# One hybrid decoder step: moving the recurrence stage's elementwise work between GpSimd, VectorE and ScalarE

## The chip, the cores and the metric

The kernel runs on one core of a Trainium2 chip. The metric is the device time in microseconds (us) of one execution, so smaller is better. Five engines work side by side and each takes its own instructions strictly in order: TensorE (PE in the rows, with its weight loads as PEld), VectorE (DVE), ScalarE (ACT), GpSimd (POOL) and SyncE (SP), which issues most of the transfers. An instruction that waits for a semaphore holds back everything behind it on its engine.

## The reference

One prompt of 512 tokens and 8 single-token samples (520 columns in all) pass a recurrent layer (HGRN2) with an MLP, then a sliding-window attention layer with an MLP. Only the recurrent layer is touched:

```python
q, f, i, g = jnp.split(h @ w_in, 4, axis=-1)
q = jax.nn.silu(q)
fg = lb + (1.0 - lb) * jax.nn.sigmoid(f)
o, S = _hgrn2_scan(heads(q), heads(1.0 - fg), heads(i), heads(jnp.log(fg)), s0)
o = _rms_norm(o, gn_g) * jax.nn.silu(heads(g))
return o.reshape(b, L, D_MODEL) @ w_out, S
# one step of the scan, for each of 8 heads of 128:
# S_new = exp(last) * S + k^T v;  o = causal part within the block + q S
```

For a sample one step of the same recurrence is taken: its stored state is scaled by the forget value, the outer product of key and value is added, the result is stored (output `hg_s`) and read by the query.

## The kernel before, in words

All matrices are fp32 and every product is made in three matmuls: weights and activations are split into an upper and a lower half, and upper x upper, upper x lower, lower x upper are added up in PSUM (`mm_half`, L229; 8 rows of 128 inputs, so 24 matmuls for each half of the columns; the two halves are 256 and 264 columns wide, in banks `ps_a` and `ps_b`). `split_w` makes the halves of a weight tile: ScalarE copies it into the rounded upper half (L179), and VectorE or GpSimd subtracts that from the raw tile to get the lower half (L180, `wsp<-wraw,wsp`, 128 x 1024 elements).

In order of time the program has a set-up (up to some 50 us), the loop over the 8 heads of the recurrence (up to some 316 us), the output gates and the output projection, a norm, the first MLP (from 404 us), attention, and the second MLP. In the loop, each head has

- `proj_head`: three weight tiles (`proj`): forget gate, query, value. The forget gate goes through a sigmoid (L422), then E = sigmoid x scale + bias (L423) and KQ = 1 - E (L424); the query through L427 and L428; the value is copied by L430. Small pieces for the samples are copied by GpSimd (L436 to L440).
- `scan_head`: the block-wise scan. VectorE doubles the block size seven times (QK in L467, E in L469); TensorE makes the small products (L449), masked into `diag` (L461, L472); ScalarE copies the pieces into `att` (L484 to L489); L491, L494, L496 turn the keys, L499 makes the states, L504 chains them, L515 and L517 make the output, and L519 to L527 normalize it: square, sum, power -0.5 on GpSimd (L523), product, and a transposition on TensorE (L527).
- after every second head `sample_pair`: the stored states of two heads for 8 samples come into one buffer, `Ss`, which exists once (L534); L541 spreads the value over the samples (`vx`); L543 scales the states; L547 and L549 add the new product; the states go out (L550); L555 to L559 make the output, L562 its square sum, L564 the power, L565 the scaling of `od`, L567 a transposition.

The order of the instructions on each engine is fixed when the program is built: a scheduler of the framework simulates the engines with its own costs and takes what is ready, so TensorE's work of the next head's projections (L229) is filled in between the small products of the scan of this head. Weights come through two raw buffers (`wraw`) and three split ones (`wsp`); the next pair's states can only be loaded into `Ss` when the last pair's have been stored and read.

Of the kernel before, what the change touches and what calls it, by code (L numbers as in the profile page):

```python
# [11 lines left out]
AF = mybir.ActivationFunctionType  # L12
ALU = mybir.AluOpType
AX = mybir.AxisListType

P = 128
# [26 lines left out]
def yoco_kernel(ctx: ExitStack, tc: tile.TileContext, I, O, dbg=None):  # L43
# [52 lines left out]
    def bc(ap, axis, n):  # L96
        a = ap.unsqueeze(axis)
        s = list(a.shape)
        s[axis] = n
        return a.broadcast_to(s)  # L100
# [106 lines left out]
    def load_w(src, raw=None):  # L207

        nk, cols = src.shape[0] // P, src.shape[1]
        raw = (wp.tile([P, 2048], F32, name="wraw") if raw is None else raw)[:, 0:nk * cols].rearrange("p (k f) -> p k f", k=nk)  # L210
        sp.dma_start(out=raw, in_=src.rearrange("(k p) f -> p k f", p=P))
        return raw

    def split_w(raw, lo_eng=None, w=None):
        nk, cols = raw.shape[1], raw.shape[2]
        if w is None:
            w = wp.tile([P, 2, 1024], F32R, name="wsp", bufs=WB)[:, :, 0:nk * cols]
        w = w.rearrange("p s (k f) -> p s k f", k=nk)
        split_into(w[:, 0], w[:, 1], raw, lo_eng)
        return w  # L220
# [164 lines left out]
    with ExitStack() as st:  # L385
# [20 lines left out]

        def proj(grp, head, act_A):
            if first and grp < 2:
                w = split_w(first.pop(0), None if grp else pool)
            else:  # L410
                w = split_w(load_w(win[:, grp * D + head * P:grp * D + (head + 1) * P]), pool)
            for h in range(2):
                yield HALVES[h], mm_half(w, act_A, h)

        def proj_head(hd):
            KQ = hg2.tile([P, 2, T], F32, name="KQ")
            E = hg2.tile([P, 2, T], F32, name="E")
            V = hg2.tile([P, T], F32, name="V")
            pool.memset(E[:, 0, 0:L], 1.0)
            for (a, b), m in proj(1, hd, A):  # L420
                s = hg2.tile([P, 264], F32, name="sg")[:, 0:b - a]
                act.activation(s, m, AF.Sigmoid)  # L422
                dve.tensor_scalar(E[:, 1, a:b], s, lbt[:, 1, hd:hd + 1], lbt[:, 0, hd:hd + 1], ALU.mult, ALU.add)  # L423
                dve.tensor_scalar(KQ[:, 0, a:b], E[:, 1, a:b], -1.0, 1.0, ALU.mult, ALU.add)  # L424
            for (a, b), m in proj(0, hd, A):
                s = hg2.tile([P, 264], F32, name="sg")[:, 0:b - a]
                act.activation(s, m, AF.Sigmoid)  # L427
                dve.tensor_tensor(KQ[:, 1, a:b], m, s, ALU.mult)  # L428
            for (a, b), m in proj(2, hd, A):
                act.copy(V[:, a:b], m)  # L430
            i, (skv, sq), fs = hd % 2, smps[hd // 2 % 2], fss[hd // 2 % 2]
            sh = hg2.tile([P, 2, NS], F32R, name="sh")
            for z, src in enumerate((KQ[:, 0, L:T], V[:, L:T])):
                hi = sh[:, z].bitcast(F32)
                g = skv[:, z, i, :, 0:NS]
                pool.tensor_copy(sh[:, z], src)  # L436
                pool.tensor_copy((g[:, 0:2], g[:, 0::2])[z], bc(hi, 1, 2))
                pool.tensor_tensor((g[:, 2:4], g[:, 1::2])[z], bc(src, 1, 2), bc(hi, 1, 2), ALU.subtract)
            pool.tensor_copy(sq[:, i, 0:NS], KQ[:, 1, L:T])
            pool.tensor_copy(fs[:, i, :], E[:, 1, L:T])  # L440
            return KQ, E, V
# [10 lines left out]
        def scan_head(h, KQ, E, V):  # L452
# [63 lines left out]
                if c:  # L516
                    pe.matmul(po[:, cs], KQ[:, 1, cs], S[:, c - 1], start=False, stop=True)  # L517
            sq = hg2.tile([P, NB, P], F32, name="osq", bufs=1)
            act.activation(sq, po.rearrange("p (c v) -> p c v", c=NB), AF.Square)  # L519
            ms = hg2.tile([P, NB], F32, name="oms")  # L520
            dve.tensor_reduce(ms, sq, axis=AX.X, op=ALU.add)
            dve.tensor_scalar(ms, ms, 1.0 / P, EPS, ALU.mult, ALU.add)
            pool.tensor_tensor(ms, ms, expo[:, 0:NB], ALU.pow)  # L523
            dve.tensor_tensor(sq, po.rearrange("p (c v) -> p c v", c=NB), bc(ms, 2, P), ALU.mult)
# [5 lines left out]
        def sample_pair(p):  # L530
            (skv, sq), fs = smps[p % 2], fss[p % 2]
            S = hg.tile([P, 2, NS, P], F32, name="Ss")
            for i in range(2):
                sp.dma_start(out=S[:, i], in_=I["state_hgrn"][0, :, 2 * p + i].rearrange("b d v -> d b v"))  # L534
            tp = ps1()
            for z in range(2):
                pe.transpose(out=tp[:, z * P:(z + 1) * P], in_=skv[:, z].rearrange("p i g b -> p (i g b)"), identity=ident)
            kT = hg2.tile([P, P], F32R, name="skT", bufs=1)
            act.copy(kT, tp[:, 0:P])
            vx = hg2.tile([P, NS, P], F32R, name="vx", bufs=1)  # L540
            dve.tensor_tensor(vx, bc(tp[:, P:2 * P], 1, NS), bc(dlt[:, 0:8], 2, P), ALU.mult)  # L541
            for i in range(2):
                pool.tensor_tensor(S[:, i], S[:, i], bc(fs[:, i], 2, P), ALU.mult)  # L543
                r = slice(64 * i, 64 * i + 64)
                for b in range(2):
                    kv = ps1()
                    pe.matmul(kv, kT[r, :], vx[r, 4 * b:4 * b + 4, :], start=True, stop=True)  # L547
                    sv = S[:, i, 4 * b:4 * b + 4, :]
                    dve.tensor_tensor(sv, sv, kv.rearrange("p (b v) -> p b v", b=4), ALU.add)  # L549
                sp.dma_start(out=O["hg_s"][0, :, 2 * p + i].rearrange("b d v -> d b v"), in_=S[:, i])  # L550
            po = ps1()
            for i in range(2):
                for b in range(2):
                    r = 64 * i + 32 * b
                    pe.matmul(po[r:r + 32, :], sq[:, i, :], S[:, i, 4 * b:4 * b + 4, :], start=True, stop=True)  # L555
            oo = hg2.tile([P, 4, P], F32, name="oo", bufs=1)
            dve.tensor_tensor(oo, po.rearrange("p (b v) -> p b v", b=4), bc(dlt[:, 8:12], 2, P), ALU.mult)
            od = hg2.tile([P, P], F32, name="od", bufs=1)
            dve.tensor_reduce(od, oo.rearrange("p b v -> p v b"), axis=AX.X, op=ALU.add)  # L559
            osq = hg2.tile([P, P], F32, name="odq", bufs=1)  # L560
            ms = hg2.tile([P, 1], F32, name="odm")
            act.activation(osq, od, AF.Square, accum_out=ms)  # L562
            dve.tensor_scalar(ms, ms, 1.0 / P, EPS, ALU.mult, ALU.add)
            pool.tensor_tensor(ms, ms, expo[:, 0:1], ALU.pow)  # L564
            dve.tensor_scalar(od, od, ms, None, ALU.mult)  # L565
            pt = ps1()
            pe.transpose(out=pt[:, 0:P], in_=od, identity=ident)  # L567
            act.activation(o32[:, 2 * p:2 * p + 2, L:T].rearrange("p i (c r) -> p i c r", c=2),
                           _ap(pt, 0, [[64, 2], [36, 2], [1, 4]]), AF.Copy, scale=GN)
# [435 lines left out]
```

## Time and profile before

| | |
|---|---|
| three runs | 1404.94, 1406.4, 1407.34 us (median 1406.4) |
| the profiled execution | 1405.58 us, of which the span from first to last instruction is 1403.8 |
| TensorE busy in the span | 1354.4 us (96%), mean granted clock 0.989 |
| VectorE, ScalarE, GpSimd busy | 819.6 us (58%), 536.1 (38%), 303.4 (22%) |
| transfers | 186 MB, 133 GB/s over the span |

The busy shares are means over stages with very different limits. The granted clock is TensorE's, as a share of full speed. Times of instructions and waits come from the one profiled execution.

### The profile page before, as it was taken

How to read it: one execution, taken by the hardware profiler on the slowest of the kernel's cores; microseconds unless marked ns; L12 is line 12 of the kernel's file. 1: busy time of each engine (PE TensorE's matmuls, PEld its weight loads, DVE VectorE, ACT ScalarE, POOL GpSimd, SP SyncE). 2: the span in 40 equal slices, each digit the busy share in tenths (PEclk: the TensorE clock that was granted, in tenths of full speed). 3: DMA queues.
4: the chain of work that ended last, by engine and by line, in shares of the span. 5: the costliest groups of instructions: out<-in, count | busy, mean ns of one | idle time of the engine just before them, and what ended most of it. 6: DMA issues, size and time to landing. Idle time of an engine off the chain costs nothing.

```text
span 1403.8 us, 29513 instructions
## 1 busy us (share of the span) xinstructions
PE 1354.4 (96%) x12459; PEld 1245.3 (89%) x12459; DVE 819.6 (58%) x1667; ACT 536.1 (38%) x1160; POOL 303.4 (22%) x315
## 2 busy tenths in 40 slices
PE   6899999899999999999999999999999999999998
PEld 4688878789889999999999966888889999999998
DVE  5676876864694443444446786777664544444432
ACT  4333333334453322322314454656454413324222
POOL 1534553353150000000000475534430000000000
PEclk9999999999999999999999999999999999999999
DMA  9744465434654552643644564113311323232231
GB/s 340 203 132 131 119 181 153 122 97 161 224 158 142 171 197 67 210 150 92 212 147 141 172 227 129 54 39 96 123 31 61 120 91 91 91 91 91 91 106 47
DMA packets 185974, 186.04 MB, mean 133 GB/s; under 512 B 6945, under 2 KB 156394, under 8 KB 185842
## 3 DMA queue, kind: packets, MB, share of 16 engines
q1 hardware_dynamic: 185600, 184.07, 41.3%
q8 instruction: 98, 1.61, 0.5%
q14 instruction: 34, 0.28, 0.1%
q10 hardware_dynamic: 242, 0.08, 0.0%
HBM read 177.00 MB, written 9.21 MB: 133 GB/s over the span
## 4 chain that ended last, share of the span: by engine, by line
PE 82%; DVE 9%; DMA 3%; issue 2%; ACT 2%; POOL 1%; SPq 0%; ACTq 0%; POOLq 0%; DVEq 0%
PE ps_b L229 34%; PE ps_a L229 32%; PE ps_a L682 4%; PE ps_e L122 3%; DVE E L469 1%; PE ps_b L768 1%; DVE QK L467 1%; PE ps_d L806 1%; DMA wraw<-in_hg_w_in_dram 1%; DVE h L187 1%; DMA adaw<-in_w_ada_dram 1%; PE ps_c L449 1%; DVE acc L155 1%; PE ps_d L499 1%; DVE X L241 1%
## 5 line engine op out<-in xcount | busy, mean ns | idle before, releaser
L229 PEld LDWEIGHTS ps_a<-A,wsp 128*128 128x128 f32 x2424 | 300.2, 192 | 28.7 <-issue 11.0
L229 PE MATMUL ps_a<-A,wsp 128*128 128x256 f32 x2424 | 319.0, 287 | 6.8 <-ACT A L193 2.6
L229 PE MATMUL ps_b<-A,wsp 128*128 128x264 f32 x2424 | 317.0, 286 | 0.8 <-DVE A L180 0.8
L229 PEld LDWEIGHTS ps_b<-A,wsp 128*128 128x128 f32 x2424 | 301.8, 189 | 10.4 <-issue 7.3
L179 ACT CAST wsp<-wraw 128x1024 fp32r<-128x1024 f32 (+1 forms) x193 | 197.9, 1027 | 284.2 <-PE ps_b L229 240.1
L180 DVE TENSOR_TENSOR wsp<-wraw,wsp 128x1024 fp32r<-128x1024 f32 (+1 forms) x159 | 193.6, 1219 | 59.9 <-ACT wsp L179 59.8
L229 PE MATMUL ps_b<-u,wsp 128*128 128x264 f32 x1536 | 200.7, 285 | 0.0
L229 PEld LDWEIGHTS ps_b<-u,wsp 128*128 128x128 f32 x1536 | 192.0, 188 | 0.1
L229 PE MATMUL ps_a<-u,wsp 128*128 128x256 f32 x1536 | 191.8, 281 | 0.1
L229 PEld LDWEIGHTS ps_a<-u,wsp 128*128 128x128 f32 x1536 | 186.0, 188 | 2.9 <-ACT u L179 2.5
L272 DVE TENSOR_TENSOR rl<-rl 128x264 f32<-128x264 f32 (+1 forms) x128 | 54.7, 428 | 135.5 <-ACT rl L271 135.5
L237 DVE SCALAR_TENSOR_TENSOR X<-ps_b,MOD,X 128x256 f32<-128x256 f32 x88 | 42.3, 481 | 135.9 <-PE ps_b L229 135.7
L171 POOL TENSOR_TENSOR rs<-rs,expo 128x2 f32<-128x2 f32 (+1 forms) x8 | 6.5, 814 | 406.1 <-DVE rs L170 401.8
L180 POOL TENSOR_TENSOR wsp<-wraw,wsp 128x1024 fp32r<-128x1024 f32 x34 | 84.1, 2475 | 32.2 <-ACT wsp L179 31.8
L237 DVE SCALAR_TENSOR_TENSOR X<-ps_a,MOD,X 128x256 f32<-128x256 f32 x88 | 42.3, 481 | 54.2 <-PE ps_a L229 54.0
L180 DVE TENSOR_TENSOR u<-rl,u 128x264 fp32r<-128x264 f32 (+1 forms) x128 | 56.8, 445 | 27.6 <-ACT u L179 27.4
L682 PE MATMUL ps_a<-wsp,u 128*128 128x256 f32 (+1 forms) x480 | 66.7, 287 | 2.1 <-ACT Vt L690 1.3
L682 PEld LDWEIGHTS ps_a<-wsp,u 128*128 128x128 f32 (+1 forms) x480 | 55.7, 168 | 12.0 <-issue 3.2
L179 ACT CAST u<-rl 128x264 fp32r<-128x264 f32 (+1 forms) x128 | 52.1, 408 | 33.7 <-DVE rl L272 33.7
L469 DVE TENSOR_TENSOR E<-E 128x512 f32<-128x512 f32 x56 | 61.0, 1090 | 0.7
L271 ACT ACTIVATE rl<-ps_a 128x256 f32<-128x256 f32 x64 | 24.5, 384 | 94.3 <-PE ps_a L229 94.3
L271 ACT ACTIVATE rl<-ps_b 128x264 f32<-128x264 f32 x64 | 25.0, 392 | 92.3 <-PE ps_b L229 92.3
(289 smaller groups left out, 1547.3 us busy)
## 6 DMA issues: line engine op xcount, KB each, us to landing
adaw<-in_w_ada_dram SPq DMA_DIRECT2D x36, 1024.0 KB
wraw<-in_w_down_dram SPq DMA_DIRECT2D x36, 1024.0 KB
wraw<-in_w_up_dram SPq DMA_DIRECT2D x32, 1024.0 KB
wraw<-in_hg_w_in_dram SPq DMA_DIRECT2D x32, 512.0 KB
wraw<-in_w_ada_dram SPq DMA_DIRECT2D x12, 1024.0 KB
wraw<-in_hg_w_out_dram SPq DMA_DIRECT2D x8, 1024.0 KB
adaw<-in_kv_w_ada_dram SPq DMA_DIRECT2D x8, 1024.0 KB
Ss<-in_state_hgrn_dram SPq DMA_DIRECT2D x8, 512.0 KB
```

Source lines behind the costliest of these rows:

```text
L122: pe.matmul(acc_ps[32 * kk:32 * kk + 32, :], cT[:, i, 4 * r + kk, :], wt[:, kk, :], start=(i == 0 and r == 0), stop=(i == n - 1 and r == 1))
L155: dve.tensor_tensor(acc[:, a:b], acc[:, a:b], sq[:, 0:b - a], ALU.add)
L179: act.copy(dst_hi, src)
L180: (lo_eng or dve).tensor_tensor(dst_lo, src, dst_hi.bitcast(F32), ALU.subtract)
L187: dve.scalar_tensor_tensor(t, X[:, j, a:a + 256], MOD[:, va, j, 8:9], rb[:, 0:256], ALU.mult, ALU.mult)
L229: pe.matmul(m[:, 0:b - a], w[:, wi, k, :], A[:, ai, k0 + k, a:b], start=(k == 0 and wi == 0 and ai == 0), stop=(k == nk - 1 and wi == 1))
L237: dve.scalar_tensor_tensor(xv, m[:, 0:256], MOD[:, vg, j, 8:9], xv, ALU.mult, ALU.add)
L241: dve.tensor_tensor(X[:, j, L:T], X[:, j, L:T], t, ALU.add)
L271: act.activation(r, m, AF.Relu)
L272: dve.tensor_tensor(r, r, r, ALU.mult)
L469: dve.tensor_tensor(_ap(E, 0, dims), _ap(E, 0, dims), tot, ALU.mult)
L682: pe.matmul(m[0:nr, 0:256], A[:, ai, k, cs], w[k][:, wi, :], start=(k == 0 and ai == 0 and wi == 0), stop=(k == KT - 1 and ai == 1))
```

## The change

Five pieces of elementwise work in the loop over heads get another engine. Nothing else of the program is edited, but the scheduler orders the engines anew.

```diff
         def proj(grp, head, act_A):
             if first and grp < 2:
-                w = split_w(first.pop(0), None if grp else pool)
+                w = split_w(first.pop(0))
             else:
-                w = split_w(load_w(win[:, grp * D + head * P:grp * D + (head + 1) * P]), pool)
+                w = split_w(load_w(win[:, grp * D + head * P:grp * D + (head + 1) * P]))
...
-                dve.tensor_scalar(E[:, 1, a:b], s, lbt[:, 1, hd:hd + 1], lbt[:, 0, hd:hd + 1], ALU.mult, ALU.add)
-                dve.tensor_scalar(KQ[:, 0, a:b], E[:, 1, a:b], -1.0, 1.0, ALU.mult, ALU.add)
+                act.activation(E[:, 1, a:b], s, AF.Identity, scale=lbt[:, 1, hd:hd + 1], bias=lbt[:, 0, hd:hd + 1])
+                act.activation(KQ[:, 0, a:b], E[:, 1, a:b], AF.Identity, scale=-1.0, bias=ones[:, 0:1])
...
-            act.activation(sq, po.rearrange("p (c v) -> p c v", c=NB), AF.Square)
-            dve.tensor_reduce(ms, sq, axis=AX.X, op=ALU.add)
+            for c in range(NB):
+                act.activation(sq[:, c], po[:, c * P:(c + 1) * P], AF.Square, accum_out=ms[:, c:c + 1])
...
-            dve.tensor_tensor(vx, bc(tp[:, P:2 * P], 1, NS), bc(dlt[:, 0:8], 2, P), ALU.mult)
+            for b in range(NS):
+                act.activation(vx[:, b], tp[:, P:2 * P], AF.Copy, scale=dlt[:, b:b + 1])
             for i in range(2):
-                pool.tensor_tensor(S[:, i], S[:, i], bc(fs[:, i], 2, P), ALU.mult)
+                for b in range(NS):
+                    act.activation(S[:, i, b], S[:, i, b], AF.Copy, scale=fs[:, i, b:b + 1])
...
-            dve.tensor_scalar(od, od, ms, None, ALU.mult)
+            act.activation(od, od, AF.Copy, scale=ms)
```

The new program has three more lines, so L543, L547, L549, L555, L562, L564, L565 and L567 of before are L545, L549, L551, L557, L564, L566, L567 and L569 of the new one.

The first place is VectorE at the start of the first head's scan. Before:

```order
L423 TENSOR_SCALAR E<-sg,lbt 128x264
L428 TENSOR_TENSOR KQ<-ps_a,sg 128x256
L424 TENSOR_SCALAR KQ<-E 128x264
L428 TENSOR_TENSOR KQ<-ps_b,sg 128x264
L467 TENSOR_TENSOR QK<-KQ,E 128x512
L469 TENSOR_TENSOR E<-E 128x256x2
L467 TENSOR_TENSOR QK<-KQ,E 128x512
L469 TENSOR_TENSOR E<-E 128x128x2x2
L461 TENSOR_TENSOR diag<-ps_c,masks 128x128
L467 TENSOR_TENSOR QK<-KQ,E 128x512
L472 COPY_PREDICATED diag<-masks,ps_c 128x128
```

Now:

```order
L428 TENSOR_TENSOR KQ<-ps_a,sg 128x256
L180 TENSOR_TENSOR wsp<-wraw,wsp 128x1024
L428 TENSOR_TENSOR KQ<-ps_b,sg 128x264
L467 TENSOR_TENSOR QK<-KQ,E 128x512
L180 TENSOR_TENSOR wsp<-wraw,wsp 128x1024
L469 TENSOR_TENSOR E<-E 128x256x2
L461 TENSOR_TENSOR diag<-ps_c,masks 128x128
L467 TENSOR_TENSOR QK<-KQ,E 128x512
L472 COPY_PREDICATED diag<-masks,ps_c 128x128
L469 TENSOR_TENSOR E<-E 128x128x2x2
L180 TENSOR_TENSOR wsp<-wraw,wsp 128x1024
```

The products of E and KQ (L423, L424) are gone from the row, three lower halves of weights (L180) stand in it, and the first masked product (L461) has one doubling step (L467, L469) ahead of it where it had two.

The second place is ScalarE after the first pair of samples (heads 0 and 1), where the square sum of the samples' output is made. Before:

```order
L528 ACTIVATE o_406<-ps_d,GT 128x512
L459 COPY vts<-ps_d 128x512
L562 ACTIVATE odq,odm<-od 128x128
L422 ACTIVATE sg<-ps_a 128x256
L568 ACTIVATE o_406<-ps_e,GT 128x2x8
L489 COPY att_426<-diag 32x4x32 x4
L422 ACTIVATE sg<-ps_b 128x264
L179 CAST wsp<-wraw 128x1024
```

Now:

```order
L528 ACTIVATE o_406<-ps_d,GT 128x512
L564 ACTIVATE odq,odm<-od 128x128
L545 ACTIVATE Ss<-Ss,fs_424 128x128 x8
L459 COPY vts<-ps_d 128x512
L545 ACTIVATE Ss<-Ss,fs_424 128x128
L567 ACTIVATE od<-od,odm 128x128
L545 ACTIVATE Ss<-Ss,fs_424 128x128 x7
L422 ACTIVATE sg<-ps_a 128x256
L570 ACTIVATE o_406<-ps_e,GT 128x2x8
```

The scaling of the samples' output (`od`, L567 now) has come to ScalarE, and so have the scalings of the next pair's states (L545, 8 for each half of `Ss`); nine of these stand ahead of the output's scaling, seven behind it and ahead of the next head's sigmoid.

The third place is TensorE in the same stretch, from the product that reads the samples' states (L555 before, L557 now) to the transposition of their output (L567, L569). Before:

```order
L555 MATMUL ps_e<-Ss,sq_416 32x512 x4
L449 MATMUL ps_c<-QK 32x32 x2
L229 MATMUL ps_a<-A,wsp 128x256 x12
L457 MATMUL ps_d<-ident,V 128x128 x4
L449 MATMUL ps_c<-QK 32x32 x32
L229 MATMUL ps_a<-A,wsp 128x256 x12
L229 MATMUL ps_b<-A,wsp 128x264 x7
L449 MATMUL ps_c<-QK 32x32 x8
L567 MATMUL ps_e<-ident,od 128x128
```

Now:

```order
L557 MATMUL ps_e<-Ss,sq_416 32x512 x4
L449 MATMUL ps_c<-KQ 32x32 x4
L527 MATMUL ps_d<-ident,osq 128x128 x4
L449 MATMUL ps_c<-KQ 32x32 x6
L449 MATMUL ps_c<-QK 32x32 x16
L229 MATMUL ps_a<-A,wsp 128x256 x19
L457 MATMUL ps_d<-ident,V 128x128 x4
L229 MATMUL ps_a<-A,wsp 128x256 x5
L229 MATMUL ps_b<-A,wsp 128x264 x4
L449 MATMUL ps_c<-QK 32x32 x32
L229 MATMUL ps_b<-A,wsp 128x264 x17
L449 MATMUL ps_c<-QK 32x32 x4
L569 MATMUL ps_e<-ident,od 128x128
```

Between the two stand 31 matmuls of the projections (L229) before and 45 now. Of the second and third pair it is 21 and 49 before, 42 and 62 now. In ScalarE's row one scaling of the next pair's states stands ahead of the output's scaling after the second pair, and six, with four squares of the norm, after the third.

## Rows read from the trace of the kernel before

**Rows 1.** Windows by stage, in us: each engine busy, instructions, granted clock, DMA
```profile
core 0: us, PE busy (x) PEld busy (x) DVE busy (x) ACT busy (x) POOL busy (x), PEclk, DMA share, GB/s
50.00:72.00 22.00, 18.96 (x301) 17.04 (x300) 16.69 (x21) 5.50 (x10) 14.23 (x13) 0.85 0.57 179
72.00:316.00 244.00, 231.85 (x3152) 203.06 (x3139) 179.50 (x299) 82.99 (x187) 110.13 (x112) 1.00 0.46 133
404.00:1403.00 999.00, 984.51 (x8169) 924.79 (x8168) 537.70 (x1181) 381.88 (x850) 136.46 (x143) 0.99 0.37 118
```

**Rows 2.** Chain that ended last, gates stage: start us, us, what
```profile
318.20 2.91 PE ps_b L229 x24
```

**Rows 3.** Waits of PE, 49 to 316 us: total us, times, longest us
```profile
PE ps_e L567 <- DVE od L565: 4.2, 2, 3.2
PE ps_d L494 <- DVE KQ L491: 2.3, 3, 1.5
PE ps_c L449 <- DVE diag L461: 2.2, 1, 2.2
PE ps_d L527 <- DVE osq L524: 1.9, 2, 1.4
PE ps_e L547 <- DVE Ss L549: 1.9, 2, 1.5
```

**Rows 4.** Groups by form, 40 to 460 us: busy us, mean ns | idle before
```profile
L180 POOL TENSOR_TENSOR wsp<-wraw,wsp 128x1024 fp32r<-128x1024 f32 x31 | 76.7, 2475 | 13.0 <-ACT wsp L179 12.7
L180 DVE TENSOR_TENSOR wsp<-wraw,wsp 128x1024 fp32r<-128x1024 f32 x22 | 27.3, 1245 | 7.4 <-ACT wsp L179 7.4
L543 POOL TENSOR_TENSOR Ss<-Ss,fs 128x1024 f32<-128x1024 f32 x8 | 16.1, 2021 | 21.0 <-DMA Ss<-in_state_hgrn_dram 20.9
L423 DVE TENSOR_SCALAR E<-sg,lbt 128x264 f32<-128x264 f32 x8 | 3.3, 413 | 11.6 <-ACT sg L422 11.6
L521 DVE TENSOR_REDUCE oms<-osq 128x4 f32<-128x512 f32 x8 | 5.4, 674 | 5.4 <-ACT osq L519 5.4
L541 DVE TENSOR_TENSOR vx<-ps_e,dlt 128x1024 fp32r<-128x1024 f32 x4 | 4.9, 1216 | 0.5 <-ACT skT L539 0.5
```

**Rows 5.** Timelines of DVE and POOL: start us, us, engine, line, operation
```profile
25.99 2.66 DVE L194 SCALAR_TENSOR_TENSOR A<-h,MOD,A 128x256 fp32r<-128x256 f32 x2 [0.85 <-ACT A L193]
32.02 0.87 DVE L194 SCALAR_TENSOR_TENSOR A<-h,MOD,A 128x256 fp32r<-128x256 f32 x2
113.92 3.37 DVE L469 TENSOR_TENSOR E<-E 128x512 f32<-128x512 f32 x1
118.42 0.69 DVE L469 TENSOR_TENSOR E<-E 128x512 f32<-128x512 f32 x1
113.91 2.39 POOL L180 TENSOR_TENSOR wsp<-wraw,wsp 128x1024 fp32r<-128x1024 f32 x1
```

**Rows 6.** Timeline around one pair of samples (heads 4 and 5)
```profile
255.42 0.38 SPq L550 DMA_DIRECT2D out_hg_s_dram<-Ss  x1
259.87 0.99 SPq L534 DMA_DIRECT2D Ss<-in_state_hgrn_dram  x2
260.32 0.31 ACT L562 ACTIVATE odq<-od 128x128 f32<-128x128 f32 x1 [5.78 <-DVE od L559]
264.88 1.90 POOL L543 TENSOR_TENSOR Ss<-Ss,fs 128x1024 f32<-128x1024 f32 x1 [15.29 <-DMA Ss<-in_state_hgrn_dram]
269.73 0.33 PE L567 MATMUL ps_e<-ident,od 128*128 128x128 f32 x1 [3.18 <-DVE od L565]
```

**Rows 7.** Single ScalarE instructions: by form, and one from the timeline
```profile
L154 ACT ACTIVATE sq<-X 128x264 f32<-128x264 f32 x7 | 2.7, 416 | 7.6 <-DVE X L241 4.2 <-DVE acc L155 3.4
L190 ACT ACTIVATE h<-h,MOD 128x256 f32<-128x256 f32 x12 | 5.9, 505 | 2.3 <-DVE h L187 2.1
L502 ACT COPY S<-ps_d 128x128 f32<-128x128 f32 x8 | 2.1, 267 | 13.8 <-PE ps_d L499 11.8 <-issue 2.0
156.49 0.19 ACT L562 ACTIVATION_READ_ACCUMULATOR odq<-od 128x1 f32 x1
```


## The prediction

> **What bounds it now.** I read the windows by stage first. From 404 us to the end TensorE is busy 984.5 of 999 us, so nothing can be won there; in the loop over heads it is busy 18.96 of 22 us (50 to 72) and 231.85 of 244 us (72 to 316), which leaves 3.04 + 12.15 = 15.2 us idle [rows 1]. That, and a lower clock in the first of the two windows, is all that the change can win in the loop. What TensorE does there isn't touched. The gates stage behind it is matmuls without a gap, 24 of them in 2.91 us (0.12 us each) in the chain that ended last [rows 2], and the order of the engines differs little there.
>
> Next, the waits of TensorE in the loop. The largest are all for VectorE: 4.2 us for the scaling of the samples' output (L565), 2.3 for the keys (L491), 2.2 for the first masked product (L461), 1.9 for the norm's product (L524), 1.9 for the states' sum (L549) [rows 3]. So VectorE is late at a few places, though it isn't full.
>
> Why it is late stands in the timelines. The doubling step L469 takes 0.69 us at 118.42, but 3.37 us at 113.92, and in that time, from 113.91, GpSimd makes a lower half (L180) for 2.39 us [rows 5]. The same is seen in the set-up: two instructions of L194 take 2.66 us at 25.99 and 0.87 at 32.02 [rows 5]. So here VectorE instructions with two operands in SBUF stand still while GpSimd reads SBUF. The Trainium skill says the same ("SBUF — State Buffer", Who interferes with whom: VectorE's second input comes through a read port shared with GpSimd, and one of the two is fully blocked for the whole instruction). By that rule the new subtractions on VectorE, which have two SBUF inputs, can in turn hold up GpSimd's short copies and powers; rival D takes that up, with a price from rows.
>
> **Part by part.**
>
> Lower halves. GpSimd makes 31 of them at 2.475 us between 40 and 460 us, 29 of them in the loop; VectorE takes 1.245 us for the same [rows 4]. So VectorE gets 29 x 1.245 = 36 us of work, and GpSimd is rid of 29 x 2.475 = 72 us. With GpSimd's state scalings (8 x 2.02 = 16 us [rows 4]) gone as well, hardly anything long is left there to hold VectorE up.
>
> E, KQ, the norm's sum, `vx`, `od`. VectorE is rid of 32 instructions of E and KQ at up to 0.41 us (13 us), of 5.4 us of L521 and of 4.9 us of L541 [rows 4]: 23 us, against 36 added. Its own work grows by 13 us on 196 us busy of 266 [rows 1], but in these 196 the blocked time is counted as busy.
>
> The waits for VectorE. The wait of 2.2 us at L461 surely goes: the order now has one doubling step and one subtraction ahead of it (0.69 + 1.245 us), where two steps stood that were held up by GpSimd. For the others (2.3 + 1.9 + 1.9) [rows 3] I assume that they go too, as the instructions ahead of them are no longer blocked, and hold back 1.0 for the subtractions that stand ahead of something now and for the longer norm: four squares with their read-out take 4 x (0.31 + 0.19) = 2.0 us [rows 6, 7] and replace a square and a reduction of 0.67 [rows 4], so at most 1.3 us more for each head. 8.3 - 1.0 = **-7.3 us**; bounds -8.3 and 0.
>
> Clock. In 50 to 72 us the granted clock is 0.85, from 72 us on it is 1.00 [rows 1]: TensorE ran partly at 1.2 instead of 2.4 GHz, in the stretch in which it waited for L461. At full clock 22 us would be 0.15 x 22 = 3.3 us shorter. Part of it hangs on the set-up before, which stays. Half: **-1.6 us**; bounds -3.3 and 0.
>
> Set-up. The two blocked instructions lose 2.66 - 0.87 = 1.8 us [rows 5]; a subtraction of 1.245 us [rows 4] takes GpSimd's place on the same engine in this stretch. **-0.5 us**; bounds -1.8 and +1.2.
>
> ScalarE's new work. No row of before shows a 128-wide copy with a scale from a pointer. A plain one from PSUM takes 0.267 us; a pointer adds 0.505 - 0.416 = 0.09 (L190 and L154, about as wide) [rows 7]. So 0.36 us each: 64 scalings of states 23 us, 32 of `vx` 11.5, 32 of E and KQ at 0.5 us 16, the norm 8 x 1.4 = 11, `od` 1.4: 63 us on 88.5 busy of 266 [rows 1], some 57%. ScalarE is not full. E and KQ each get about 0.1 us slower (0.505 against 0.413 [rows 4, 7]); the 48 matmuls of the query's projection, 5.75 us [rows 2], lie between them and the scan, so nothing. `vx` takes 8 x 0.36 = 2.9 us instead of 1.2 [rows 4]; the projections that are filled in cover it, and bare it would cost 4 x 1.7 = 6.8 us. The Trainium skill ("ScalarE: Activation LUTs", What ACT_TABLE_LOAD costs) gives 186 ns + 0.833 ns for each element, 93 ns for each pointer, and 93 ns of overlap back to back: 293 ns. The trace agrees on the pointer (0.09 us). By the page the 17.3 us of scalings that come up below would be 48 x 0.293 = 14.1, and the eighth that I take of them 1.8 instead of 2.2: 0.4 us off the sum.
>
> The samples' wait, now on ScalarE. This is the dearest step, and the one with a cost. The states of the next pair can be loaded when the last ones are stored: in rows 6 the store is issued at 255.42, the loads at 259.87, and GpSimd, which had waited 15.29 us, starts to scale at 264.88, so 9.5 us after the store [rows 6]. Now ScalarE stands there, and behind it, in order, stands the scaling of `od`, which TensorE waits for. By the order there are nine scalings and a copy ahead of it after the first pair, one after the second, six and four squares after the third: `od` is ready some 13.3, 10.1 and 13.6 us after the store (scalings at 0.36, the squares at 0.5 us each, and the copy of `vts`, 512 wide, at 0.6, an estimate from the 128 and 264 columns of [rows 7]). TensorE came to L567 11.1 us after the store in rows 6 (269.73 - 3.18 - 255.42); 49 matmuls of the projections make 5.9 us of it and 5.2 are other work. Some of that other work stands elsewhere in the new order; I take 4.0 (between 5.2 and half of it). With 45, 42 and 62 matmuls at 0.12 us TensorE arrives after 9.4, 9.0 and 11.4 us and waits 3.9 + 1.1 + 2.2 = 7.2 us; with 5.2 it would be 3.6, with 2.6 11.4. Against 4.2 us for L565 now [rows 3]: **+3.0 us**.
>
> Behind that stand ScalarE's sigmoids, key copies and `att` copies, late by the 16 scalings, 5.8 us at three places, 17.3 us together. A projection of both halves keeps TensorE busy for 5.75 us [rows 2], about as long, so little comes through; I take an eighth: **+2.2 us**; bounds 0 and 17.3. Samples together +5.2; bounds -4.2 and +24.5 (7.2 + 17.3 on top).
>
> Sum: -7.3 - 1.6 - 0.5 + 5.2 = -4.2 us. The profiled execution took 1405.58 us, 1.8 around its span of 1403.8, and lies 0.8 below the median of the runs. 1405.6 - 4.2 = **1401.4 us**.
>
> **Rivals.**
>
> B, the samples' wait is hidden: the state comes earlier or TensorE later than I have it, and ScalarE catches up. Then the 4.2 us of L565 go as well and nothing comes back: -7.3 - 1.6 - 0.5 - 4.2 = -13.6, 1392.0 us. For it: GpSimd's scaling was late by no more than the transfer, and ScalarE is half empty. Against it: `od` is now behind a transfer of which the trace shows 9.5 us.
>
> C, ScalarE becomes the wait: three quarters of the 17.3 us come through, because the sigmoids that free a PSUM bank and the copies that feed the states (L499) and outputs (L515) stand behind the scalings. -9.4 + 3.0 + 13.0 = +6.6, 1412.2 us. It decides for slower (over 2.8 us, 0.2%, which is about what a measurement can tell from no change) from a share of (2.8 + 9.4 - 3.0) / 17.3 = 0.53. For it: the row of ScalarE, with seven scalings ahead of the next sigmoid. Against it: two banks and 5.75 us of matmuls for each projection. A rule of the Trainium skill speaks for this side ("ScalarE: Activation LUTs", Rules for kernel authors): additions and products belong on VectorE rather than ScalarE. The rows agree on the sizes: 8 pieces of 0.36 us against 1.216 for `vx` [rows 4].
>
> D, the freed time comes back in VectorE's row: 29 subtractions of 1.245 us stand ahead of scan steps and block GpSimd's powers, which cost the norm the same. Half of the 7.3 is lost, the clock gains nothing: -3.6 - 0.5 + 5.2 = +1.1, 1406.7 us. For it: VectorE's own work grows by 13 us. Against it: a blocked L469 costs 2.7 us, a subtraction 1.2.
>
> **Numbers.** A (forecast) 0.41, B 0.21, D 0.18, C 0.20. Faster takes A and B, 0.62; same D, 0.18; slower C, 0.20. The range reaches from just under B to C, 1389 to 1412; it leaves out half of C and the far end of B. The forecast's own range, with the samples' term between +1 and +7, is 1397 to 1403.
>
> **What would show it.** Right: L469 has one duration near 0.7 us; the waits for L461, L491 and L524 are gone; TensorE's largest wait in the loop is L569 for ScalarE's L567, three times 1 to 4 us; ScalarE waits for the transfer into `Ss` at L545; the clock in 50 to 72 us is nearer 1. Wrong, towards C: waits of TensorE for ScalarE at L229 (sigmoid), L499 or L515 of more than some 9 us together. Wrong, towards D: L461, L491 and L524 still waited for. Towards B: no wait at L569. A loss behind 404 us would be something that I have not seen, as TensorE has no gap there.

## The result, and the profile after

The changed kernel takes 1387.43 us (median of 4 runs, 1384.12 to 1392.95), the kernel before 1405.67 (4 runs): a ratio of 0.9875, 95% interval 0.9838 to 0.9913, 18.2 us faster. The forecast was 4.2 us. The profiled execution took 1385.64 us with a span of 1383.9, which is 19.9 us shorter than the span of before.

The page splits these 19.9 us at once: TensorE is busy 1348.5 us where it was 1354.4, with the same 12459 matmuls (5.9 us, which I put down to the clock: 0.996 where it was 0.989), and idle 35.4 us where it was 49.4 (14.0 us). The line of the page, first of before, then of now:

```profile
PE 1354.4 (96%) x12459; PEld 1245.3 (89%) x12459; DVE 819.6 (58%) x1667; ACT 536.1 (38%) x1160; POOL 303.4 (22%) x315
PE 1348.5 (97%) x12459; PEld 1239.5 (90%) x12459; DVE 795.5 (57%) x1650; ACT 581.6 (42%) x1348; POOL 214.9 (16%) x276
```

Windows by stage of the changed kernel, columns as in [rows 1]; the loop ends some 16 us earlier now, so the third window ends at 300:

```profile
20.00:50.00 30.00, 23.85 (x173) 15.97 (x173) 19.59 (x53) 14.47 (x29) 2.60 (x8) 0.94 1.00 306
50.00:72.00 22.00, 21.72 (x346) 19.60 (x345) 17.14 (x27) 15.23 (x39) 7.14 (x13) 1.00 0.63 192
72.00:300.00 228.00, 224.94 (x3059) 195.44 (x3058) 152.72 (x270) 117.46 (x343) 37.44 (x77) 1.00 0.48 141
390.00:1384.00 994.00, 978.30 (x8154) 919.61 (x8152) 536.73 (x1181) 380.76 (x848) 135.28 (x142) 1.00 0.37 118
```

In the loop TensorE is idle 0.28 + 3.06 = 3.3 us, against 15.2 in [rows 1]: 11.9 of the 14.0 us are won there. GpSimd has fallen from 14.23 to 7.14 us in the first of these windows, and the clock in it has risen from 0.85 to 1.00. ScalarE has become busier (117.46 us) and is still half empty.

The waits of TensorE from 49 to 300 us (total us, times, longest), to be set against [rows 3]:

```profile
PE ps_e L122 <- DMA adaw<-in_w_ada_dram: 1.9, 2, 1.4
PE ps_e L569 <- ACT od L567: 0.7, 2, 0.6
PE ps_c L449 <- DVE QK L467: 0.3, 1, 0.3
PE ps_e L130 <- ACT o L570: 0.3, 1, 0.3
```

All five waits of [rows 3] are gone but for 0.7 us of the samples' output (L567 before, L569 now). The largest wait is now for a transfer, the modulation weights (`adaw`).

The groups by form (busy us, mean ns):

```profile
L180 DVE TENSOR_TENSOR wsp<-wraw,wsp 128x1024 fp32r<-128x1024 f32 x52 | 64.4, 1240 | 21.0 <-ACT wsp L179 20.4 <-PE ps_e L569 0.4
L469 DVE TENSOR_TENSOR E<-E 128x512 f32<-128x512 f32 x56 | 42.8, 764 | 0.7
L545 ACT ACTIVATE Ss<-Ss,fs 128x128 f32<-128x128 f32 x64 | 19.9, 392 | 4.8 <-DMA Ss<-in_state_hgrn_dram 4.6 <-POOL fs L440 0.2
L423 ACT ACTIVATE E<-sg,lbt 128x264 f32<-128x264 f32 x8 | 4.9, 608 | 0.1
L521 ACT ACTIVATE osq<-ps_c 128x128 f32<-128x128 f32 x32 | 8.4, 276 | 12.7 <-PE ps_c L517 12.7
```

The doubling step L469 has a mean of 0.764 us, near the undisturbed 0.69 of [rows 5]. Before, single ones took up to 3.37 us, and the mean was 1.090:

```profile
L469 DVE TENSOR_TENSOR E<-E 128x512 f32<-128x512 f32 x56 | 61.0, 1090 | 0.7
```

E (L423) takes 0.61 us on ScalarE where it took 0.41 on VectorE [rows 4]; GpSimd's small copies wait for it, TensorE does not.

The stretch after the pair of heads 4 and 5, which answers to [rows 6] (start us, us, engine, line):

```profile
249.06 0.38 SPq L552 DMA_DIRECT2D out_hg_s_dram<-Ss  x1
252.82 1.00 SPq L534 DMA_DIRECT2D Ss<-in_state_hgrn_dram  x2
257.16 1.87 ACT L545 ACTIVATE Ss<-Ss,fs 128x128 f32<-128x128 f32 x6 [0.85 <-DMA Ss<-in_state_hgrn_dram]
259.93 0.40 ACT L567 ACTIVATE od<-od,odm 128x128 f32<-128x128 f32 x1
261.65 0.33 PE L569 MATMUL ps_e<-ident,od 128*128 128x128 f32 x1
```

The order is the one foreseen: ScalarE waits for the states, scales six of them, and only then scales `od`. But the states are there 8.1 us after the store (9.5 in [rows 6]), six scalings take 1.87 us (0.31 each), `od` is ready after 11.3 us, and TensorE comes only after 12.6: no wait.

### The profile page after: what moved, and what is told of

It reads as the page before. It is cut to its first block, busy times and chain, and to the rows that moved or that the text cites. A ratio compares the mean times of both kernels' runs of the same rounds, so it can differ in the third digit from the quotient of the medians.

```text
span 1383.9 us, 29621 instructions
## 1 busy us (share of the span) xinstructions
PE 1348.5 (97%) x12459; PEld 1239.5 (90%) x12459; DVE 795.5 (57%) x1650; ACT 581.6 (42%) x1348; POOL 214.9 (16%) x276
## 4 chain that ended last, share of the span: by engine, by line
PE 82%; DMA 7%; DVE 6%; ACT 2%; issue 1%; POOL 1%; SPq 0%; ACTq 0%; DVEq 0%; POOLq 0%
PE ps_b L229 34%; PE ps_a L229 32%; PE ps_a L684 4%; PE ps_e L122 3%; DMA wraw<-in_hg_w_in_dram 2%; DMA adaw<-in_w_ada_dram 1%; DVE wsp L180 1%; DMA wraw<-in_w_up_dram 1%; PE ps_b L770 1%; PE ps_c L449 1%; DVE h L187 1%; DMA wraw<-in_w_o_dram 1%; DVE acc L155 1%; DMA Ss<-in_state_hgrn_dram 1%; ACT wsp L179 1%
## 5 line engine op out<-in xcount | busy, mean ns | idle before, releaser
L229 PE MATMUL ps_a<-A,wsp 128*128 128x256 f32 x2424 | 316.5, 285 | 7.4 <-ACT A L193 2.4
L229 PEld LDWEIGHTS ps_a<-A,wsp 128*128 128x128 f32 x2424 | 297.1, 190 | 27.5 <-issue 7.5
L229 PE MATMUL ps_b<-A,wsp 128*128 128x264 f32 x2424 | 315.0, 285 | 0.0
L229 PEld LDWEIGHTS ps_b<-A,wsp 128*128 128x128 f32 x2424 | 300.3, 188 | 10.0 <-issue 8.7
L180 DVE TENSOR_TENSOR wsp<-wraw,wsp 128x1024 fp32r<-128x1024 f32 (+1 forms) x190 | 232.4, 1224 | 75.1 <-ACT wsp L179 74.4
L229 PE MATMUL ps_b<-u,wsp 128*128 128x264 f32 x1536 | 200.7, 285 | 0.0
L229 PEld LDWEIGHTS ps_b<-u,wsp 128*128 128x128 f32 x1536 | 192.0, 188 | 0.1
L229 PE MATMUL ps_a<-u,wsp 128*128 128x256 f32 x1536 | 191.8, 281 | 0.1
L229 PEld LDWEIGHTS ps_a<-u,wsp 128*128 128x128 f32 x1536 | 185.9, 188 | 2.9 <-ACT u L179 1.7
L180 DVE TENSOR_TENSOR u<-rl,u 128x264 fp32r<-128x264 f32 (+1 forms) x128 | 56.8, 445 | 27.6 <-ACT u L179 27.4
L469 DVE TENSOR_TENSOR E<-E 128x512 f32<-128x512 f32 x56 | 42.8, 764 | 0.7
L122 PE MATMUL ps_e<-adaw,cT 128*32 128x512 f32 x288 | 40.5, 601 | 2.5 <-DMA adaw<-in_w_ada_dram 1.9
```

The source lines that it names most:

```text
L122: pe.matmul(acc_ps[32 * kk:32 * kk + 32, :], cT[:, i, 4 * r + kk, :], wt[:, kk, :], start=(i == 0 and r == 0), stop=(i == n - 1 and r == 1))
L180: (lo_eng or dve).tensor_tensor(dst_lo, src, dst_hi.bitcast(F32), ALU.subtract)
L229: pe.matmul(m[:, 0:b - a], w[:, wi, k, :], A[:, ai, k0 + k, a:b], start=(k == 0 and wi == 0 and ai == 0), stop=(k == nk - 1 and wi == 1))
L469: dve.tensor_tensor(_ap(E, 0, dims), _ap(E, 0, dims), tot, ALU.mult)
```

## The experiments

Theory 1: the time came from VectorE being blocked by GpSimd's long reads of SBUF, and taking these reads away gave it back. Theory 2, the rival: VectorE was short of time, and its work that went to ScalarE gave it back. A third question is the step of the prediction that was to cost 5.2 us: states and samples' output on ScalarE. Each kernel was timed in several rounds against the kernel before on the same chip, whose median was 1403.9 to 1405.6 us.

**The parts alone.** `sub_only` has only the two lines of the lower halves:

```diff
-                w = split_w(first.pop(0), None if grp else pool)
+                w = split_w(first.pop(0))
...
-                w = split_w(load_w(win[:, grp * D + head * P:grp * D + (head + 1) * P]), pool)
+                w = split_w(load_w(win[:, grp * D + head * P:grp * D + (head + 1) * P]))
```

> The kernel before with only the lower halves of the weights moved from GpSimd to VectorE. Theory 1 (GpSimd's long reads of SBUF block VectorE): 72 of the 88 us of such reads in the loop are gone, so most of the change's gain is there already: 1391 to 1397 us, L469 mean near 0.75 us, and the waits of TensorE for VectorE in the loop under 3 us together. Theory 2 (VectorE gains because its own work goes to ScalarE): VectorE has 36 us more to do, so no gain, 1403 us or more.

Measured: 1397.73 us, ratio 0.9949 (0.993 to 0.9968); L469 0.803 us. VectorE has gained though it has more to do, against theory 2; but 7 us are less than theory 1 gave it, and the waits for VectorE in the loop are 8.3 us where it wanted under 3. The waits of TensorE:

```profile
PE ps_e L122 <- DMA adaw<-in_w_ada_dram: 6.6, 4, 3.2
PE ps_c L478 <- DVE QK L467: 4.2, 2, 2.7
PE ps_e L537 <- DVE adared L132: 2.1, 1, 2.1
PE ps_e L567 <- DVE od L565: 1.6, 2, 1.4
PE ps_d L494 <- DVE KQ L491: 0.4, 1, 0.4
```

The largest is for the modulation weights; that is taken up below. `act_only` is the changed kernel with that diff undone.

> The changed kernel with the lower halves of the weights left on GpSimd (all that goes to ScalarE is moved). Theory 1: only the state scalings (16 us of 88 us of long reads on GpSimd) are gone, L469 stays near 1.05 us, gain 2 to 6 us: 1400 to 1404 us. Theory 2: most of the gain, 1395 us or less.

Measured: 1401.7 us, 0.998 (0.9968 to 0.9992), L469 1.015 us: as theory 1 has it.

**More reads, more writes.** The direct test takes the changed kernel and gives GpSimd useless work at the moments at which it made the lower halves. `pool_reads` (1024 columns), `pool_half` (the same with 512) and `pool_writes`, where `upper` is written here for the upper half of the weight tile, `w[:, 0]`:

```diff
+                if grp < 3:   # pool_reads
+                    pool.tensor_tensor(scr, upper, upper, ALU.subtract)
...
+                if grp < 3:   # pool_writes
+                    pool.tensor_copy(scr[:, 0:8], upper[:, 0:8])
+                    for _ in range(2):
+                        pool.memset(scr, 0.0)
```

> The changed kernel with one more GpSimd instruction for each weight tile of the loop, which subtracts the upper half (128 x 1024, read from SBUF) from itself into a scratch tile that nobody reads; 22 of them, some 2.4 us each. Theory 1: VectorE is blocked again, L469 mean 0.95 us or more, 4 to 10 us slower than the changed kernel: 1391 to 1398 us. Theory 2: nothing waits for the scratch tile, so the time of the changed kernel within 3 us (1384 to 1391).

> As the run with the extra reads, but the extra work of GpSimd only writes: for each weight tile a copy of 8 columns (which ties it to the same moment) and two memsets of 128 x 1024 into the scratch tile. Theory 1: writes do not block VectorE's reads, L469 mean stays under 0.8 us, and the time is that of the changed kernel within 3 us (1384 to 1391). A third theory (GpSimd's own late copies and powers cost the time, not blocked reads) expects it as slow as the run with the reads.

Measured: 1403.74 us with the reads, 0.9993 (0.9982 to 1.0004), so the whole gain is gone; 1390.59 with the writes, 0.9901 (0.9883 to 0.9919). The order of the instructions on TensorE and VectorE is the same in both but for 20 and 1 of them, so the two can be set against each other; against the changed kernel some 210 and 36 stand elsewhere in either. Groups by form, first of the reads, then of the writes:

```profile
L414 POOL TENSOR_TENSOR scr<-wsp 128x1024 f32<-128x1024 f32 x22 | 50.9, 2312 | 67.3 <-ACT wsp L179 67.3
L472 DVE TENSOR_TENSOR E<-E 128x512 f32<-128x512 f32 x56 | 49.6, 886 | 0.7
L180 DVE TENSOR_TENSOR wsp<-wraw,wsp 128x1024 fp32r<-128x1024 f32 x50 | 78.0, 1564 | 21.5 <-ACT wsp L179 21.1 <-PE ps_e L572 0.4
```

```profile
L474 DVE TENSOR_TENSOR E<-E 128x512 f32<-128x512 f32 x56 | 42.9, 766 | 0.8
L180 DVE TENSOR_TENSOR wsp<-wraw,wsp 128x1024 fp32r<-128x1024 f32 x52 | 65.7, 1268 | 24.2 <-ACT wsp L179 21.6 <-POOL skv L443 2.0 <-PE ps_e L574 0.4
L416 POOL MEMSET scr<- 128x1024 f32 x44 | 41.9, 953 | 2.2
L414 POOL COPY scr<-wsp 128x8 f32<-128x8 f32 x22 | 13.9, 632 | 62.1 <-ACT wsp L179 61.9
```

With 50.9 us of reads the doubling step is slowed to 0.886 us, with 41.9 + 13.9 = 55.8 us of writes and tiny copies it stays at 0.766. The reads slow the lower halves (L180) more, from 1.268 to 1.564 us, and QK from 0.707 to 0.811: over the three lines VectorE loses some 27 us. So it is the reads, not GpSimd's busy time, and theory 3 (GpSimd's own late powers) falls with theory 2: VectorE's wait for GpSimd's power in the norm is 1.8 us with the reads and 2.5 with the writes. The slowing of the doubling step is less than foreseen (0.95), the price more (15 to 16 us against the changed kernel, not 4 to 10).

> As the run with the extra reads of GpSimd, but each reads 512 columns instead of 1024 (some 1.2 us instead of 2.3). Theory 1: half of the blocked time, 5 to 11 us slower than the changed kernel, 1393 to 1398, as long as VectorE has no room that hides short stops; if it has, under 3 us.

Measured: 1392.71 us, 0.9905 (0.9883 to 0.9926), 4.3 above the changed kernel on the same chip (1388.46), between the two expectations. Half the length of a read costs about a quarter by the medians, but the two intervals overlap. In its trace the same three lines of VectorE lose some 12 us where they lost 27, so part of the shorter stops may be hidden; that was not tested further.

**Which moves count beside the lower halves.** `sub_states` moves the lower halves and the states' scaling only, `no_states` all but the states' scaling:

```diff
-                for b in range(NS):
-                    act.activation(S[:, i, b], S[:, i, b], AF.Copy, scale=fs[:, i, b:b + 1])
+                pool.tensor_tensor(S[:, i], S[:, i], bc(fs[:, i], 2, P), ALU.mult)
```

> The lower halves on VectorE and the state scalings on ScalarE; E, KQ, the norm's sum, vx and the samples' output stay on VectorE, so that GpSimd has no long read of SBUF left in the loop but VectorE keeps 23 us of its own work. Theory 1 alone (only blocked reads count): as the changed kernel within 3 us, 1385 to 1391. Theory 1 with 2 (the lower halves moved to VectorE need the room that the moves to ScalarE make there): 5 to 10 us slower than the changed kernel, 1393 to 1398.

> The changed kernel with the state scalings left on GpSimd (8 reads of some 2 us). Theory 1: the 22 extra reads of 2.3 us cost 16 us, 0.7 us each, so 8 cost 4 to 6 us: 1391 to 1394 us. The prediction's step on the samples (scaling on ScalarE puts the wait for the transfer ahead of the samples' output and costs 5.2 us) expects this kernel faster than the changed one, 1380 to 1385.

Measured: `sub_states` 1388.07 us, 0.9893 (0.9874 to 0.9912), `no_states` 1389.58, 0.9894 (0.9877 to 0.991). Both are the changed kernel within what can be told. The first is theory 1 alone. The second neither confirms the step on the samples (which wanted 1380 to 1385) nor gives the eight reads the price that I had for them.

**The samples on ScalarE.** Four times as many scalings (pieces of 32 columns), two buffers for the states, and the output's scaling back on VectorE:

```diff
+                    for q in range(4):   # states_x4, each piece 32 columns
...
-            S = hg.tile([P, 2, NS, P], F32, name="Ss")
+            S = hg.tile([P, 2, NS, P], F32, name="Ss", bufs=2)   # ss_two
...
-            act.activation(od, od, AF.Copy, scale=ms)
+            dve.tensor_scalar(od, od, ms, None, ALU.mult)   # od_dve
```

> The changed kernel with each scaling of a state in four pieces of 32 columns: 256 instructions at some 0.2 us (an estimate from 0.31 us for 128 columns) instead of 64, some 30 us more on ScalarE, 8 us behind each transfer. If ScalarE's room covers its scalings (what the changed kernel's trace looks like), within 4 us of the changed kernel. If rival C was near (the sigmoids and copies behind the scalings reach TensorE), 8 to 20 us slower, with waits of TensorE for ScalarE.

> The changed kernel with two buffers for the samples' states, so that the next pair's states are loaded long before ScalarE comes to scale them. The prediction's step on the samples would expect the whole 5 us back, 1380 to 1384. The trace of the changed kernel, in which TensorE waits 0.7 us at L569, expects no more than 1 us: 1385 to 1389.

> The changed kernel with the scaling of the samples' output left on VectorE, so that it no longer stands behind the state scalings on ScalarE. The prediction's step on the samples expects the 7.2 us of waits at L569 gone, 4 to 7 us faster. The trace of the changed kernel (0.7 us at L569) expects it within 2 us.

Measured: `states_x4` 1402.39 us, 0.9982 (0.9969 to 0.9994). The scalings take 57.4 us of ScalarE instead of 19.9, and the kernel loses some 14. Waits of TensorE in the loop:

```profile
PE ps_e L122 <- DMA adaw<-in_w_ada_dram: 4.0, 3, 1.7
PE ps_e L570 <- ACT od L568: 3.0, 2, 2.1
PE ps_e L550 <- ACT vx L542: 2.8, 2, 1.8
PE ps_e L550 <- DVE Ss L552: 1.6, 2, 0.8
```

So rival C was a real danger, 37 us of ScalarE work away. `ss_two` took 1381.73 us, 0.9837 (0.982 to 0.9853), in the range in which the prediction's step was to give its 5 us back (1380 to 1384); but the changed kernel had not run beside it. So both ran once more, beside `od_dve`:

> The changed kernel once more, on the same chip as the next three, so that they can be set against it: 1384 to 1391 us, and the spread of its runs over some 4 us or more.

> The changed kernel with two buffers for the samples' states, beside the changed kernel. If the wait for the transfer on ScalarE still costs what the prediction gave it, 4 to 6 us faster than the changed kernel. If the first run's 1381.7 us was mostly the chip and the clock (its trace is 0.8 us ahead of the changed kernel's at the end), within 2 us of it.

Measured on one chip: changed kernel 1388.46 us, 0.9882 (0.9858 to 0.9905); two buffers 1384.25, 0.985 (0.9827 to 0.9873); `od_dve` 1386.68, 0.9866 (0.9844 to 0.9888). The output's scaling costs nothing measurable on ScalarE. Two buffers gain some 4 us by the medians, as the expectation of a wait on ScalarE had it; but the changed kernel's trace has only 0.6 us of waits at L569 to give, so most of it must come from elsewhere.

**What TensorE waits for now.** The second profiled execution of the changed kernel was slower, with a span of 1390.6 us. Its waits, three of its windows between 200 and 220 us, and the 24 matmuls behind the first wait, in this execution and then in the faster one:

```profile
PE ps_e L122 <- DMA adaw<-in_w_ada_dram: 4.8, 3, 2.4
PE ps_e L569 <- ACT od L567: 0.6, 1, 0.6
```

```profile
200.00:205.00 5.00, 5.00 (x44) 4.82 (x45) 1.29 (x2) 0.43 (x2) 0.06 (x1) 0.66 0.67 223
205.00:210.00 5.00, 5.00 (x140) 3.81 (x138) 3.17 (x7) 2.07 (x3) 0.57 (x3) 1.00 0.26 73
215.00:220.00 5.00, 3.96 (x23) 2.89 (x24) 0.75 (x1) 0.71 (x3) 0.00 (x0) 0.73 0.33 88
```

```profile
199.83 4.71 PE L229 MATMUL ps_b<-A,wsp 128*128 128x264 f32 x24
196.52 3.18 PE L229 MATMUL ps_b<-A,wsp 128*128 128x264 f32 x24
```

TensorE waits for the modulation weights, which have one buffer in the loop. Behind two of these waits (2.41 us before 198.83, 1.96 us before 216.04) the granted clock falls to 0.66 and 0.73, that is, part of the five microseconds runs at 1.2 GHz. In the faster execution the same waits were 1.9 us together, the longest 1.4, and the clock there stayed at 1.00. `ada_two` takes a second buffer in turns:

```diff
+        two = [adas["p"], open_pool(st, "adaA2", 1)]
+
+        class Turns:
+            def tile(self, *a, **k):
+                two.append(two.pop(0))
+                return two[0].tile(*a, **k)
+        adas["p"] = Turns()
```

> The changed kernel with a second buffer for the modulation weights of the loop (adaw), whose late transfers TensorE waits for (1.9 us in one profiled execution of the changed kernel, 4.8 in another, with the clock fallen behind it). If this transfer is what bounds the loop now and spreads its runs, the waits at L122 go, 2 to 6 us faster than the changed kernel's 1388, and the runs lie closer together. If the waits only move to the next late transfer (weights, states), within 2 us.

> Only the lower halves moved to VectorE, with a second buffer for the modulation weights. The run without it was 1397.7 us, with 6.6 us of waits for these weights. If its shortfall of 9 us against the changed kernel is that transfer, 1389 to 1393. If it is VectorE, blocked by the eight state scalings that stay on GpSimd and full of its own work, 1395 us or more, with waits for VectorE.

Measured: `ada_two` 1384.4 us, 0.986 (0.9843 to 0.9876), four runs from 1384.08 to 1385.14, where the changed kernel's spread over 6 to 9 us. That is the gain expected, but not shown beyond doubt: the changed kernel did not run beside it, the intervals of the ratios overlap, and in the trace the waits for the transfer are gone from the loop while 3.8 us of others stand there. The lower halves alone with that buffer: 1382.2 us, 0.9846 (0.9832 to 0.9861), 15 us better than without it and better than either expectation. What TensorE still waits for in the loop of that kernel:

```profile
PE ps_e L574 <- DVE od L572: 1.2, 1, 1.2
PE ps_c L456 <- DVE QK L474: 0.4, 1, 0.4
PE ps_b L229 <- issue: 0.2, 1, 0.2
```

The waits of 4.2 and 2.1 us for VectorE in `sub_only` are gone with those for the transfer, though VectorE still has all its own work and GpSimd its eight state scalings. The buffer also makes the scheduler order the engines anew (151 of VectorE's 1698 instructions stand elsewhere than in `sub_only`), so transfer and order are not told apart here. The last three put the buffer into the other kernels:

> The kernel before with only the second buffer for the modulation weights. If GpSimd's reads are the cause on their own, VectorE stays late and the gain is about the 1.2 us of waits for these weights that its trace shows: 1402 to 1404.5 us. If the late transfer was behind the waits for VectorE as well, 1395 us or less.

> Only the moves to ScalarE, with the second buffer for the modulation weights. Theory 1: GpSimd still makes 29 lower halves, VectorE stays blocked, at most 3 us off the 1401.7 us without the buffer: 1398 to 1402. If the single buffer had hidden what ScalarE's moves are worth (as it did with the lower halves, 1397.7 to 1382.2), 1392 us or less.

> The lower halves to VectorE, the state scalings to ScalarE, and the second buffer. If GpSimd's last eight long reads still cost something, under 1381 us. If TensorE's remaining waits lie elsewhere (set-up, clock), 1381 to 1385 like the two other kernels with that buffer.

Measured: kernel before with the buffer 1403.29 us, 1.0 (0.9987 to 1.0013); moves to ScalarE alone with it 1403.57, 1.0004 (0.9991 to 1.0017); lower halves and states 1385.48, 0.9865 (0.9848 to 0.9883), with runs from 1383.17 to 1390.41. The second and the third lie just above the range expected. The buffer does nothing while GpSimd blocks VectorE, and the moves to ScalarE are worth nothing with it; the lower halves are worth 21 us (1403.29 to 1382.2, from two chips). The lower halves with the states spread over 7 us in spite of the buffer, and TensorE still waits 1.5 us for the modulation weights in its profiled execution, the slowest of the four, so the buffer does not end these waits in every order. TensorE's waits in the kernel before with the buffer:

```profile
PE ps_d L534 <- DVE osq L531: 5.1, 5, 1.4
PE ps_e L574 <- DVE od L572: 3.2, 3, 1.4
PE ps_c L456 <- DVE diag L468: 2.3, 1, 2.3
```

They are for VectorE, as in [rows 3].

## Why the prediction was right and wrong

**What bounds it: right.** Blocked VectorE instructions were the cause, and theory 1 is shown by the extra reads against the extra writes. The page "SBUF — State Buffer" of the Trainium skill (Who interferes with whom) has the rule that two SBUF operands on VectorE contend with GpSimd's reads and not with its writes; 0.886 against 0.766 us for L469 agrees.

**The waits for VectorE: right, a little small.** -7.3 us were forecast, with 1.0 held back for what the subtractions and the longer norm would put in the way. Next to nothing came back: the four waits of 8.3 us are gone, and of the smaller ones 0.3 us is left. Rival D falls.

**The samples' wait on ScalarE: the step that failed.** It was to cost 5.2 us, 7.2 of waits at L569 instead of 4.2 and 2.2 from the backlog. Measured are 0.7 us and no backlog, so it gave 3.5 us: 8.7 of the 15.7 us between the 4.2 forecast and the 19.9 measured. The mechanism is there in the trace, in the order foreseen, but its three times were off, nearly all in the direction that made a wait:

| after the store, us | heads 0, 1 | heads 2, 3 | heads 4, 5 |
|---|---|---|---|
| states there, forecast 9.5 | 7.8 | 8.1 | 8.1 |
| `od` ready, forecast 13.3, 10.1, 13.6 | 11.3 | 8.8 | 11.3 |
| TensorE there, forecast 9.4, 9.0, 11.4 | 11.2 | 8.3 | 12.6 |

I had read 9.5 us from one event, the one in [rows 6] (the other two in the trace of before are 8.5 and 9.6); there the loads were issued 4.5 us after the store and taken up 5.0 us later, now it is 3.3 to 3.9 and 4.2 to 4.6. A scaling in a row of eight takes 0.31 us, not the 0.36 that I put together from single instructions. Here the estimate of 0.293 us that the prediction worked out from the page "ScalarE: Activation LUTs" of the Trainium skill (What ACT_TABLE_LOAD costs), with its overlap of instructions back to back, was nearer. The 10.1 us should have been 9.9 by its own terms (9.5 + 0.36), which changes the wait by 0.2. And TensorE's way to L569 was guessed too short twice of three, as I took 4.0 us for its other work where the row had 5.2 (which gives 10.6, 10.3 and 12.7). Each was a microsecond or two; a wait is the difference of two such sums, and 7.2 us was made of nothing else. Rival B, 1392.0 us, was this case; it had 0.21.

**Clock and set-up: right sign, too small.** -1.6 and -0.5 us were forecast. TensorE's busy time fell by 5.9 us for the same matmuls, and its idle time outside the loop by 14.0 - 11.9 = 2.1 us, nearly all in the set-up: from 8.1 us in 20 to 50 us (the row below) to 6.2. Single instructions of L194, blocked before, take 0.5 us there now, and TensorE's wait for them fell from 1.5 to 0.7 us.

```profile
20.00:50.00 30.00, 21.89 (x148) 13.64 (x141) 20.45 (x51) 13.84 (x26) 7.65 (x10) 0.88 1.01 299
```

I had counted the clock in one window only. Behind the loop, where I said that there was nothing to win, the attention stage is also shorter: its first matmul starts at 787.17 and now at 771.35 us (15.8 apart), the last of the program at 1399.85 and 1380.35 (19.5 apart). In 20 us windows between 960 and 1040 us, three had a clock of 0.91 before and one has it now, so 2 x 0.09 x 20 = 3.6 us. The edits don't touch that stage, and other kernels here show one to three windows below 1.00 there, so I take it for chance in these executions; that was not tested.

Together: -11.9 in the loop, -2.1 of other idle time, -5.9 of clock, 19.9 us.

**Edits costed at nothing: right.** E, KQ, the norm's sum and `vx` on ScalarE cost nothing that can be seen; E takes 0.61 us, not 0.5. But they gain nothing that can be seen either, nor does the scaling of the states: with the second buffer the lower halves alone (1382.2) are no slower than the whole change (1384.4).

**What I did not see** is that a faster loop can run into the single buffer of the modulation weights. Its 1.2 us of waits were in the view from which [rows 3] come, and I left them out of the sum. In the changed kernel this is now TensorE's largest wait in the loop, and for the lower halves by themselves a second buffer, with the new order that comes with it, gives back two thirds of what they are worth. That the single buffer is what spreads the runs is not shown, as one kernel with two spreads as well. How the two buffers of `ss_two` gain 4 us stays open: its order differs in many places, its waits for the modulation weights were 2.6 to 2.8 us, and I did not separate the two.

The fastest kernels here are the lower halves on VectorE with two buffers for the modulation weights, 1382.2 us, and the changed kernel with two buffers for the states, 1381.73 and 1384.25. They can't be told apart. The first did not run beside the changed kernel; against before its interval (0.9832 to 0.9861) lies at the lower end of the changed kernel's (0.9838 to 0.9913).

## What to carry to other kernels

Look in the timeline for instructions of one form on VectorE with two very different durations, and for what GpSimd reads from SBUF in the long ones; moving that one reader was worth more than relieving VectorE of its own work. A wait that is forecast as the difference of two sums, each with an error of a microsecond or two, can be zero, so give that case its full chance. When an engine is made faster, list the transfers that TensorE already waits for a little: with one buffer they can become the next bound and hide what an edit is worth; the lower halves alone took 1397.73 us with one buffer and 1382.2 with two, though the order of the engines changed with it.

## What the runs showed that I had not expected

22 reads of 2.3 us on GpSimd cost 15 to 16 us of the kernel although L469 rose only from 0.764 to 0.886 us in the mean; more of the blocked time lies in the lower halves themselves (L180, from 1.268 us with the writes to 1.564), and reads half as long cost about 4. A transfer that came 2.4 us late cost more than its wait: the granted clock fell to 0.66 in the window of five microseconds behind it, and 24 matmuls took 4.71 us instead of 3.18. And a scaling of 32 columns on ScalarE takes 0.312 us by itself, hardly less than one of 128 columns (0.392; in the total, where the records overlap, 0.22 against 0.31 each), so cutting the states into quarters nearly tripled ScalarE's time, from 19.9 to 57.4 us.
